# A hybrid attention and recurrence layer in fp32: which copy the weight casts stand behind, and a new written order for head pairs and gates

## The chip, the cores and the metric

The kernel runs on one core of a Trainium2 chip. A core has five engines with queues of their own, each working through its instructions in order: TensorE (PE; PEld is its weight load), VectorE (DVE), ScalarE (ACT), GpSimd (POOL) and SyncE (SP). DMA transfers are issued from some of these queues and run beside them. On-chip memory is SBUF; matmuls write to banks of PSUM. The metric is the device time of one execution in microseconds (us); the median of three runs before the change is 1459.82 us.

## The reference

One layer, on an input `x` of 1024 tokens by 1024 channels, float32 throughout. A stick-breaking attention (8 heads of 64) and a gated linear recurrence (HGRN2, 4 heads of 128, chunks of 64 tokens) work side by side on the same normalised input; each is projected back, weighted by a sigmoid gate per channel, and the two are added. A squared-ReLU MLP and a last norm follow.

```python
xn = rmsnorm(x, norm1_g[layer])
u = xn @ w_in[layer].astype(f32)        # 1024 x 5632 columns
q_sb, k_sb, v_sb, f_raw, i_hg, q_hg, g_hg, gate_sb, gate_hg = jnp.split(u, list(c), axis=-1)
o_sb = merge_heads(stick_breaking_attention(...))
f = lb + (1.0 - lb) * jax.nn.sigmoid(f_raw)
o_hg = hgrn2_chunkwise(silu(q_hg), k_hg, i_hg, log(f))      # per head
o_hg = merge_heads(rmsnorm(o_hg)) * jax.nn.silu(g_hg)
g_a = jax.nn.sigmoid(gate_sb + bg[:D_MODEL])
g_b = jax.nn.sigmoid(gate_hg + bg[D_MODEL:])
merged = g_a * (o_sb @ w_o_sb) + g_b * (o_hg @ w_o_hg)
h = x + merged @ w_out[layer]
a = jnp.square(jax.nn.relu(rmsnorm(h, norm2_g) @ w_ff1))
return rmsnorm(h + a @ w_ff2, final_g)
```

## The kernel before

**Arithmetic.** A float32 product is made of three matmuls on halves of reduced precision: each operand is split into a high half `h` and a low half `l`, and `three` (its matmuls are at L121) issues h·h, h·l and l·h. A split is a cast on ACT (`hi_copy`, L148) and behind it a subtraction on DVE (`lo_sub`, L153); `hi_lo` does both. For large products the blocks of the operands are added first and multiplied in fewer products (Strassen's way): so weights are not only split but summed (`sub`, L1093), and the sums are split. A product's parts are kept as "1", "2", "X", "Y" and so on.

**Two lanes.** Up to about 540 us PE works on two lists in turns. The main lane holds the attention items and, head by head, the levels of the recurrence (for each level, multiplications on DVE by `pp`, a sum operand `sl_x`, score matmuls `sl`, and a masked copy into `sc`). The fill lane is a `Stream` named `st`: a list of jobs, each with its weight units and a body that yields after every few matmuls. `hg_jobs(h)` adds the projections of a recurrence head (`wf`, `wq`, and for even heads `wi`), `g_job(j)` the gate of a pair of heads (`wgg0`, `wgg1`), `gate_job(cb)` one block of 128 columns of both channel gates (`wga0` to `wga7`).

**A raw block** (`raw_job`; `g_job` and `gate_job` are made with it) has a unit of two raw tiles. The first is split as it is (`whi`, `wlo`). The second becomes a sum by two subtractions (`sub(rb, ra, rb)` and one of half the size), and the half of the sum is split as `t`. There are two buffers for raw tiles, and two each for `whi` and `wlo`. The body: 12 matmuls into the bank `ps`; a copy of the bank to `p1` on ACT (L1178), which a DMA on ACT's queue takes to `pd`; then `st.prefetch()`, which splits the weights of the next unit and loads those of the one after; 12 matmuls into a second bank `p4`; the sum `p14`; then 12 matmuls more into `ps`, which therefore wait for the copy; and `c11`, which makes a sigmoid of it. In `profile` rows the banks are called `pgawga` and `pgqwga`, and `p1` is `p_wga`.

**What sets the order.** The engines' orders come from a scheduler that takes instructions in written order as their inputs allow. `after(a, b)` puts instruction `a` behind `b` in this order, without a semaphore between them. `hi_lo(..., hi_behind)` uses it for a cast; `prefetch` passes the last PE instruction of the fill lane as `hi_behind` for the `whi` cast, and nothing for the `t` cast. Loads on SP's queue keep their written order (`load`).

**The gates.** `gates()` writes the last products of the gates out by hand, for two pairs of the recurrence gate (`h0`, `h1`, whose tiles carry `h`) and the eight blocks of the channel gates (`v0`, `v1`, ...). While `turns["on"]` is set, every instruction on ACT and DVE stays in the order in which it is written. A `SumPair` has `load`, `sums` (three subtractions, L1093) and `casts` (ACT casts and DVE low halves, `whig`, `wlog`, `tgh`, `tgl`); `x6`, `x7`, `y5`, `y3` are products on PE, into banks `gX` and `gY`; `x7_sums`, `y5_sum`, `y3_sum` add what earlier stages stored (`pr`, `yr`, L1090); `put(i, j)` splits a quarter of a finished operand into its halves (`ahgh`, `ahgl`).

Of the kernel before, what the change touches and what calls it, by code (L numbers as in the profile page):

```python
# [10 lines left out]
F32R = mybir.dt.float32r  # L11
# [28 lines left out]
def kernel(  # L40
# [19 lines left out]
    nc = tc.nc  # L60
# [23 lines left out]
    def bank(name):  # L84
        return psum.tile([P, 512], F32, tag="p", name=name)
# [61 lines left out]
    def hi_copy(dst, src):  # L147
        return in_turn("act", nc.scalar.copy(dst, src))  # L148

    def lo_sub(dst, src, hi):  # L150
        return in_turn(
            "dve",
            nc.vector.tensor_tensor(out=dst, in0=src, in1=hi.bitcast(F32), op=ALU.subtract),  # L153
        )

    def hi_lo(h, l, src, hi_behind=None):
        after(hi_copy(h, src), hi_behind)
        return lo_sub(l, src, h)
# [241 lines left out]
    class Unit:  # L400
# [2 lines left out]
        late = False  # L403
        roomy = ()

        def split_t(self):
            pass

        def __init__(self, name, pieces, wide=False):
# [40 lines left out]
    class Stream:  # L450
# [17 lines left out]
        def late_next(self):  # L468
            return any(u.late for us, _ in self.jobs[self.pos + 1 : self.pos + 2] for u in us)

        def prefetch(self):
            nxt = []
            for us, _ in self.jobs[self.pos + 1 :]:
                nxt += [u for u in us if u.hl is None]
                if len(nxt) >= 2:
                    break
            if nxt:
                nxt[0].split(hi_behind=lanes["fill"].last)
                nxt[0].split_t()
            if len(nxt) > 1:  # L480
                nxt[1].load()

# [22 lines left out]
    st = Stream()  # L505
# [15 lines left out]
    def proj_jobs(group, acts):  # L521


        def body():
            for half in range(2):
                if half == 1 and st.late_next():
                    st.prefetch()
                for name, unit, ep in group:
                    ps = bank(f"{name}_{half}")
                    yield from proj_half(ps, unit.hl[0], acts.mov, KT, half)  # L530
                    ep(ps, half)

        return st.add([u for _, u, _ in group], body)
# [288 lines left out]

    j_hg = {}

    def hg_jobs(h):
        for key, c0, ep in (
            ("f", C_F, f_epilogue(h)),
            ("q", C_QH, silu_epilogue(h, "q")),
        ):
            u = cols_unit(f"w{key}{h}", [(W_IN, c0 + h * P, P)])  # L830
            j_hg[h] = proj_jobs([(f"pj{key}{h}", u, ep)], xn)
        if h % 2 == 0:
            j_hg[h] = i_job(h)

# [251 lines left out]
    def half(name, dt=F32):  # L1086
        return hpool.tile([P, 512], dt, tag="h", name=name)
# [42 lines left out]
    class RawUnit(Unit):  # L1130
# [18 lines left out]
            sub(rb[:, 512:], rb[:, 512:], rb[:, 0:512])  # L1149
            self.hl = [(h, l)]  # L1150

        def split_t(self):
            if len(self.hl) == 1:
                t = slot(f"{self.name}t", F32R)
                self.hl.append((t[:, 0:512], t[:, 512:]))
                hi_lo(*self.hl[1], self.raw[1][:, 512:])

    def raw_job(name, cols, pd, c11, begin=None, middle=None):
        u = RawUnit(name, cols)

        def steps_of(ps, wt, w0, half_, k0, start):
            wh, wl = u.hl[wt]
            for k in range(4):
                c = (w0 + k) * P
                xh, xl = xn.mov(k0 + k, half_)
                three(
                    ps, wh[:, c : c + P], wl[:, c : c + P], xh, xl, start and k == 0, k == 3, True
                )
                if k % 2 == 1:
                    yield  # L1170

        def body():
            p1, p14 = (half(f"{n}_{name}") for n in ("p1", "p14"))
            ps, p4 = bank(f"pga{name}"), bank(f"pgq{name}")
            if begin:
                begin()
            yield from steps_of(ps, 0, 0, 0, 0, True)
            nc.scalar.copy(p1, ps)  # L1178
            nc.scalar.dma_start(pd[:, 0, :], p1)
            if len(u.hl) == 1:  # L1180
                u.split_t()
            st.prefetch()
            yield from steps_of(p4, 1, 0, 1, 4, True)
            add(p14, p1, p4)
            if middle:
                middle()
            nc.gpsimd.dma_start(pd[:, 1, :], p14)
            yield from steps_of(ps, 0, 4, 0, 4, False)
            c11(ps)

        return st.add([u], body)

    def gate_job(cb):
# [116 lines left out]

    j_raw, j_g = [], []
    hg_jobs(1)
    j_fill = j_hg[1]
    j_g.append(g_job(0))
    hg_jobs(2)
    j_raw += [gate_job(0), gate_job(1)]
    hg_jobs(3)
    j_g.append(g_job(1))
# [3 lines left out]
    class SumPair:  # L1322
# [26 lines left out]
            sub(r1[:, s0], r1[:, s1], r0[:, s0])  # L1349
            sub(r0[:, s1], r1[:, s1], r0[:, s1])  # L1350

        def casts(self, behind=None):
            cb = self.cb
            r0, r1 = self.raw
            s0, s1 = slice(0, 512), slice(512, 1024)
            h, l = (self.tile(t, f"{t}g{cb}", F32R) for t in ("whi", "wlo"))
            after(hi_lo(h, l, r1), behind)
            self.w = {6: (h[:, s0], l[:, s0]), 3: (h[:, s1], l[:, s1])}
            h, l = (slot(f"tg{n}{cb}", F32R) for n in "hl")
            after(hi_lo(h, l, r0), behind)  # L1360
            self.w.update({5: (h[:, s0], l[:, s0]), 7: (h[:, s1], l[:, s1])})

        def split(self, behind=None):
            self.sums()
            self.casts(behind)

        def product(self, i, ps, start):
            open_block("fill")
# [73 lines left out]
    class GatePair(SumPair):  # L1442
# [18 lines left out]
        def casts(self, behind=None):  # L1461
            super().casts(behind)
            h, l = (half(f"wo{n}{self.cb}", F32R) for n in "hl")
            hi_lo(h, l, self.wo)
            self.hg = h, l

        def hg_product(self, i):
            open_block("fill")
# [63 lines left out]
    summed = [HgPair(0), HgPair(1)] + [gp[4 * i + j] for j in range(4) for i in range(2)]  # L1532

    def gates():
        h0, h1, v0, v1 = summed[:4]
        turns.update(on=True, act=None, dve=None)
        h1.load_sums()
        h1.roomy, v0.roomy = ("whi", "wlo"), ("raw",)
        h1.sums()
        h0.first_quarter()  # L1540
        h1.casts()
# [48 lines left out]
        v0.y3_gate()  # L1590
        v0.late_half()
        v0.early_half()
        for v, n, m in zip(summed[3:], summed[4:] + [None], summed[5:] + [None] * 2):
            if v is not v1:
                v.x6()
            v.y5()
            if n:
                n.split(v.u2_sum)
# [12 lines left out]
            v.y3_sum()  # L1611
            v.y3_gate()
            v.early_half()
# [568 lines left out]
    for i, it in enumerate(items):  # L2182
# [12 lines left out]
        def between():  # L2195
            if before:
                values(*before)

        r = turn(*it, between)
# [163 lines left out]
```

## Time and profile before

| what | value |
|---|---|
| median of 3 runs | 1459.82 us (1459.38 to 1459.86) |
| the profiled execution's own time | 1457.9 us |
| its span, first to last instruction | 1456.1 us |
| mean granted TensorE clock | 0.997 |
| instructions in the profile | 19929 |
| PE waits for `p_wga` (L1178) | 4.8 us in 2 waits, the longest 4.3 us |

The profile is of one execution. Times in its rows are microseconds from the first instruction; L12 is line 12 of the kernel. A row of the timeline has start, duration, engine, line, operation, written and read tiles with buffer numbers left out (so `wga5r` is both raw tiles of that block), and in brackets how long the engine stood before it and what ended that. Matmuls are pipelined, so their durations overlap: the distance of starts is what one costs.

### The profile page before, as it was taken

To read this page: it belongs to the slowest core of one execution; us is meant where nothing else is said; L and a number is where in the kernel's file an instruction comes from. 1 tells how busy PE (TensorE), PEld (TensorE's weight loads), DVE (VectorE), ACT (ScalarE), POOL (GpSimd) and SP (SyncE) were. 2 spreads that over 40 slices of the span, in tenths; PEclk is the share of its full clock that TensorE was granted. 3 is DMA by queue.
4 is the path that set the end of the run, shared out by engine and by line. 5 is a ranking of instruction groups with operands and counts; after the bars stand their busy time and mean duration, and the time that the engine had idled before them with its cause. 6 is when DMAs were issued, how large, how long until landed. Compare 5 with 4: busy or idle time off the path is not lost. (4 is left out here: it accounts for less than half of the span.)

```text
span 1456.1 us, 19929 instructions
## 1 busy us (share of the span) xinstructions
PE 1433.2 (98%) x7418; PEld 1215.7 (83%) x7418; DVE 1114.2 (77%) x1587; ACT 685.4 (47%) x1184; POOL 127.7 (9%) x321
## 2 busy tenths in 40 slices
PE   8999999999999899999999999999999999999997
PEld 8889988988988788888888877888888888888886
DVE  6699898698577898897777798666666757768765
ACT  7566666552323344432344764444444533523433
POOL 3021111000000030000010300000000000000041
PEclk9999999999999999999999999999999999999999
DMA  7144255003034585645579413444445975676724
GB/s 207 34 120 90 57 111 109 16 23 97 20 116 108 160 224 181 203 151 179 177 265 297 159 44 131 158 158 147 158 159 180 352 261 191 247 278 244 281 102 178
DMA packets 162216, 232.01 MB, mean 159 GB/s; under 512 B 25564, under 2 KB 96264, under 8 KB 162120
## 3 DMA queue, kind: packets, MB, share of 16 engines
q1 hardware_dynamic: 146408, 187.22, 38.3%
q0 software_dynamic: 11536, 35.92, 9.5%
q10 hardware_dynamic: 4176, 7.60, 1.4%
q8 instruction: 58, 0.95, 0.3%
q14 instruction: 38, 0.31, 0.1%
HBM read 166.48 MB, written 64.23 MB: 158 GB/s over the span
## 5 line engine op out<-in xcount | busy, mean ns | idle before, releaser
L148 ACT CAST whid<-w 128x1024 fp32r<-128x1024 f32 x31 | 32.6, 1053 | 154.5 <-PE pm L121 89.9
L698 DVE TENSOR_TENSOR_SCAN rm<-rm,bits 128x511 f32<-128x511 f32 (+7 forms) x72 | 87.1, 1218 | 14.2 <-ACT rm L676 12.6
L121 PE MATMUL pm<-wlod,sh 128*128 128x512 f32 x248 | 96.6, 389 | 0.2 <-DVE wlod L153 0.2
L121 PE MATMUL pm<-whid,sl 128*128 128x512 f32 x248 | 96.5, 389 | 0.0
L121 PE MATMUL pm<-whid,sh 128*128 128x512 f32 x248 | 96.5, 389 | 0.0
L153 DVE TENSOR_TENSOR wlod<-w,whid 128x1024 fp32r<-128x1024 f32 x31 | 37.9, 1222 | 57.0 <-ACT whid L148 56.9
L121 PE MATMUL pm<-th,sl 128*128 128x512 f32 x200 | 77.8, 389 | 0.0
L121 PE MATMUL pm<-tl,sh 128*128 128x512 f32 x200 | 77.8, 389 | 0.0
L121 PE MATMUL pm<-th,sh 128*128 128x512 f32 x200 | 77.8, 389 | 0.0
L153 DVE TENSOR_TENSOR sl<-sa,sh 128x1024 fp32r<-128x1024 f32 x56 | 68.2, 1217 | 2.2 <-ACT sh L148 2.2
L148 ACT CAST wTh<-pw 128x128 fp32r<-128x128 f32 (+3 forms) x96 | 44.4, 487 | 48.7 <-PE pw L124 43.9
L148 ACT CAST sh<-sa 128x1024 fp32r<-128x1024 f32 x56 | 57.2, 1046 | 12.1 <-DMA sa<-ad 12.1
L153 DVE TENSOR_TENSOR wTl<-pw,wTh 128x512 fp32r<-128x512 f32 (+3 forms) x96 | 50.7, 547 | 9.9 <-ACT wTh L148 5.4
L121 PEld LDWEIGHTS pm<-wlod,sh 128*128 128x128 f32 x248 | 46.6, 188 | 10.3 <-DVE wlod L153 0.6
L121 PEld LDWEIGHTS pm<-whid,sh 128*128 128x128 f32 x248 | 46.5, 187 | 9.7
L121 PEld LDWEIGHTS pm<-whid,sl 128*128 128x128 f32 x248 | 46.6, 188 | 9.5
L2006 POOL TENSOR_SCALAR fss<-fss 128x1 f32<-128x1 f32 x8 | 4.4, 551 | 566.8 <-ACT fsc L2001 566.3
L161 DVE TENSOR_TENSOR bt<-bt,rm 128x511 f32<-128x511 f32 (+7 forms) x72 | 48.9, 685 | 4.4 <-ACT bt L679 0.3
L121 PE MATMUL pX<-sqh,t1l 128*128 128x512 f32 x128 | 50.1, 391 | 1.1 <-DVE t1l L153 1.1
L121 PE MATMUL pX<-sqh,t1h 128*128 128x512 f32 x128 | 50.1, 391 | 1.0 <-DVE a L1090 0.9
L676 ACT ACTIVATE rm<-z 128x511 f32<-128x511 f32 (+6 forms) x96 | 47.6, 503 | 5.2 <-DVE bt L161 1.8
L121 PE MATMUL pX<-sql,t1h 128*128 128x512 f32 x128 | 50.0, 390 | 0.0
(971 smaller groups left out, 4587.1 us busy)
## 6 DMA issues: line engine op xcount, KB each, us to landing
w<-in_w_ff_dram SPq DMA_DIRECT2D x72, 512.0 KB, 5.0
sa<-ad SPq DMA_DIRECT2D x56, 512.0 KB, 6.5
ad<-a SPq DMA_DIRECT2D x32, 256.0 KB, 2.0
ad<-s SPq DMA_DIRECT2D x16, 512.0 KB
tw<-in_w_out_dram POOLq DMA_DIRECT2D x6, 1024.0 KB, 7.7
x<-in_x_dram SPq DMA_DIRECT2D x8, 512.0 KB, 9.4
xnl<-xnh POOLq DMA_DIRECT2D x8, 512.0 KB, 10.5
pr<-pd SPq DMA_DIRECT2D x8, 512.0 KB, 6.5
```

Source lines behind the costliest of these rows:

```text
L121: return pe(nc.tensor.matmul(*a, **k))
L148: return in_turn("act", nc.scalar.copy(dst, src))
L153: nc.vector.tensor_tensor(out=dst, in0=src, in1=hi.bitcast(F32), op=ALU.subtract),
L161: return dve(nc.vector.tensor_tensor(out=out, in0=a, in1=b, op=ALU.mult))
L676: nc.scalar.activation(rm[:, s0 + c0 - 1 : s0 + m - 1], z[:, c0:m], AF.Sigmoid, scale=-0.125)
L698: sc = nc.vector.tensor_tensor_scan(out=rr, data0=rr, data1=bits[:, 1024 - nk + a : 1024 - nk + b][:, ::-1], initial=rm[:, b : b + 1] if i ...
L2006: nc.gpsimd.tensor_scalar(out=ssq, in0=ssq, scalar1=1.0 / D, scalar2=EPS, op0=ALU.mult, op1=ALU.add)
```

## The change

It has three parts.

1. **The next block's casts.** `prefetch` and `split_t` take an instruction to stand behind. `raw_job` passes the copy to `p1`, so the next unit's `whi` cast and its `t` cast, where there is one, both come behind the running block's copy in ACT's order.
2. **Head pairs.** `hg_jobs` takes a function to call between its two projections. The first `g_job` is added there, so `wgg0` stands behind `wf2` in the fill lane and on the load queue: `wf1, wq1, wf2, wgg0, wq2, wi2` for `wf1, wq1, wgg0, wf2, wq2, wi2`.
3. **The first gate blocks.** `casts` is split into `casts_hi` (ACT) and `casts_lo(n)` (DVE), and `gates()` is written in another order: the two puts `(0, 0)` ahead of `v0.sums` and `h0.x6`, `v1`'s casts ahead of `h1.x7`, `v0.y5` and `v0.y5_sum` ahead of `h1.late_times` and `h1.y3`, the other puts of `h1` earlier, and `v2`'s load, sums and casts ahead of the loop.

```diff
-        def prefetch(self):
+        def prefetch(self, behind=None):
...
             if nxt:
-                nxt[0].split(hi_behind=lanes["fill"].last)
-                nxt[0].split_t()
+                nxt[0].split(hi_behind=behind or lanes["fill"].last)
+                nxt[0].split_t(behind)
...
-    def hg_jobs(h):
+    def hg_jobs(h, between=None):
...
             j_hg[h] = proj_jobs([(f"pj{key}{h}", u, ep)], xn)
+            if between:
+                between()
+                between = None
...
-        def split_t(self):
+        def split_t(self, hi_behind=None):
...
-                hi_lo(*self.hl[1], self.raw[1][:, 512:])
+                hi_lo(*self.hl[1], self.raw[1][:, 512:], hi_behind)
...
-            nc.scalar.copy(p1, ps)
+            copied = nc.scalar.copy(p1, ps)
...
-            st.prefetch()
+            st.prefetch(copied)
...
-    j_g.append(g_job(0))
-    hg_jobs(2)
+    hg_jobs(2, lambda: j_g.append(g_job(0)))
...
-        def casts(self, behind=None):
+        def casts_hi(self):
...
+            for _, r, h in self.lows:
+                hi_copy(h, r)
+
+        def casts_lo(self, n, behind=None):
+            for _ in range(n):
+                after(lo_sub(*self.lows.pop(0)), behind)
...
         h1.first_quarter()
+        h0.put(0, 0)
+        h1.put(0, 0)
         v0.sums()
         h0.x6()
-        h0.put(0, 0)
-        h1.put(0, 0)
-        v0.casts()
+        v0.casts_hi()
+        v0.casts_lo(3)
...
         h0.early_times()
+        v1.casts_hi()
         h1.x7()
         h1.x7_sums()
+        h0.put(1, 0)
         h1.late_sigmoids()
-        h0.put(1, 0)
+        v1.casts_lo(1)
         v0.x6()
+        v1.casts_lo(2)
+        v1.load_sums()
+        v0.y5()
+        v0.y5_sum()
         h1.late_times()
-        v1.load_sums()
-        v1.casts()
         h1.y3()
         h1.y3_sum()
-        v0.y5()
-        v0.y5_sum()
         h1.put(1, 1)
+        h1.put(0, 1)
...
         v0.x7_sums()
+        h1.put(1, 0)
         v0.x7_gates()
-        h1.put(0, 1)
-        h1.put(1, 0)
         v0.y3()
-        turns["on"] = False
-        summed[4].load()
+        v2.load()
...
         v0.late_half()
+        v2.sums()
         v0.early_half()
+        v2.casts_hi()
+        turns["on"] = False
...
+            if n is v2:
+                v2.casts_lo(3, v.u2_sum)
+            elif n:
+                n.split(v.u2_sum)
```

Lines of the changed kernel behind the first of these places stand 3 lower in the file, those of the gates 9 to 18. The first place is ACT in the fourth raw block, while `wga4` runs and `wga5` is prepared. `o1` is a finished operand of the recurrence, `asbh0` a high half of the attention's output, `sc2` a masked copy of scores, `gd3` and `pd4` are DMAs. Before:

```order
L1205 DMA gd3_114<-g1_3_5398 128x512
L148 CAST wga5t_5456<-wga5r1_5344 128x512
L1052 ACTIVATE o1_4991<-pot1_1_5411,prm_91 128x512
L148 CAST asbh0_5508<-osb0_960 128x1024
L1178 COPY p1_wga4_5401<-pgawga4_5403 128x512
L148 CAST wga5whi_5450<-wga5r0_5342 128x1024
L986 COPY sc2_4959<-sl2_5_5423 32x8x32 x2
L1179 DMA pd4_107<-p1_wga4_5401 128x512
```

And now:

```order
L1208 DMA gd3_114<-g1_3_5398 128x512
L1055 ACTIVATE o1_4991<-pot1_1_5411,prm_91 128x512
L1181 COPY p1_wga4_5401<-pgawga4_5403 128x512
L148 CAST wga5whi_5450<-wga5r0_5342 128x1024
L989 COPY sc2_4959<-sl2_5_5423 32x8x32 x2
L1182 DMA pd4_107<-p1_wga4_5401 128x512
L148 CAST wga5t_5456<-wga5r1_5344 128x512
L148 CAST asbh0_5508<-osb0_960 128x1024
```

The copy `p1_wga4` stood behind the casts `wga5t` and `asbh0`; now both stand behind it, and `wga5whi` right behind it as before. The second place is DVE at the first gate blocks, ahead of PE's product `x7` of `h0`. `guh0` is the sum after which PE may go on writing `gXh`. Before:

```order
L153 TENSOR_TENSOR tglh1_6374<-wgh1r0_6356,tghh1_6373 128x1024
L161 TENSOR_TENSOR o2_5564<-o2_5564,g11r1_6362 128x512
L1093 TENSOR_TENSOR wg0r0_6377<-wg0r0_6377 128x512
L1093 TENSOR_TENSOR wg0r1_6378<-wg0r1_6378,wg0r0_6377 128x512
L1093 TENSOR_TENSOR wg0r0_6377<-wg0r1_6378,wg0r0_6377 128x512
L1090 TENSOR_TENSOR guh0_6412<-prh0_6174,gXh0_6399 128x512
L153 TENSOR_TENSOR ahgl0_6415<-o0_4340,ahgh0_6414 128x512
L153 TENSOR_TENSOR ahgl2_6419<-o2_5564,ahgh2_6418 128x512
```

And now:

```order
L153 TENSOR_TENSOR tglh1_6372<-wgh1r0_6356,tghh1_6371 128x1024
L161 TENSOR_TENSOR o2_5564<-o2_5564,g11r1_6362 128x512
L153 TENSOR_TENSOR ahgl0_6397<-o0_4340,ahgh0_6396 128x512
L153 TENSOR_TENSOR ahgl2_6401<-o2_5564,ahgh2_6400 128x512
L1096 TENSOR_TENSOR wg0r0_6377<-wg0r0_6377 128x512
L1096 TENSOR_TENSOR wg0r1_6378<-wg0r1_6378,wg0r0_6377 128x512
L1096 TENSOR_TENSOR wg0r0_6377<-wg0r1_6378,wg0r0_6377 128x512
L1093 TENSOR_TENSOR guh0_6420<-prh0_6174,gXh0_6407 128x512
```

The two low halves `ahgl0` and `ahgl2` stood behind `guh0` and now stand ahead of the sums of `wg0`, and so ahead of `guh0`. On PE, the 12 matmuls of `gY0` moved ahead of the 12 of `gYh1`'s second half. The third place is DVE at the end of the attention's last items, where the fill lane goes from head 1 to head 2. `wTl` are low halves of attention weights that PE waits for, `sd0_l` and `sl0` belong to head 0's recurrence. Before:

```order
L153 TENSOR_TENSOR wTl7_1_0_3838<-pw7_2_0_3841,wTh7_1_0_3837 128x3x128
L153 TENSOR_TENSOR sd0_l_3943<-sd0_x_3941,sd0_h_3942 128x1024
L790 TENSOR_SCALAR k1_3779<-k1_3779,oml_93 128x512
L793 TENSOR_SCALAR pp1_3778<-pp1_3778,oml_93,lb_92 128x512
L153 TENSOR_TENSOR wTl7_2_0_3792<-pw7_4_0_3861,wTh7_2_0_3791 128x4x128
L153 TENSOR_TENSOR wTl7_2_4_3794<-pw7_4_1_3868,wTh7_2_4_3793 128x128
L161 TENSOR_TENSOR q0_3074<-q0_3074,pp0_2854 128x512
L153 TENSOR_TENSOR wTl7_1_0_3838<-pw7_3_0_3885,wTh7_1_0_3837 128x4x128
L769 TENSOR_TENSOR osb3_3314<-po7_2_3892,ot7_2_3905 64x256
```

And now:

```order
L153 TENSOR_TENSOR wTl7_1_0_3836<-pw7_2_0_3839,wTh7_1_0_3835 128x3x128
L153 TENSOR_TENSOR sd0_l_3949<-sd0_x_3947,sd0_h_3948 128x1024
L153 TENSOR_TENSOR wf2l0_3871<-wf2r0_3684,wf2h0_3870 128x1024
L790 TENSOR_SCALAR k1_3777<-k1_3777,oml_93 128x512
L793 TENSOR_SCALAR pp1_3776<-pp1_3776,oml_93,lb_92 128x512
L153 TENSOR_TENSOR wTl7_2_0_3790<-pw7_4_0_3859,wTh7_2_0_3789 128x4x128
L153 TENSOR_TENSOR wTl7_2_4_3792<-pw7_4_1_3866,wTh7_2_4_3791 128x128
L161 TENSOR_TENSOR q0_3074<-q0_3074,pp0_2854 128x512
L153 TENSOR_TENSOR wTl7_1_0_3836<-pw7_3_0_3891,wTh7_1_0_3835 128x4x128
L1096 TENSOR_TENSOR wgg0r1_3876<-wgg0r0_3874,wgg0r1_3876 128x1024
L769 TENSOR_TENSOR osb3_3314<-po7_2_3898,ot7_2_3911 64x256
```

The low half `wf2l0` came into the row ahead of two of the `wTl`, and the sum `wgg0r1`, which before stood earlier than the rows shown, now stands right behind the last `wTl`. On SP's queue the load of `wf2r0` now stands ahead of those of `wgg0`.

More of the change, by code (lines that the diff above doesn't have):

```diff
@@ L1150, in split, with split_t @@
             self.hl = [(h, l)]
-        def split_t(self):
+        def split_t(self, hi_behind=None):
             if len(self.hl) == 1:
@@ L1356, in casts @@
             h, l = (self.tile(t, f"{t}g{cb}", F32R) for t in ("whi", "wlo"))
-            after(hi_lo(h, l, r1), behind)
+            self.lows = [(l, r1, h)]
             self.w = {6: (h[:, s0], l[:, s0]), 3: (h[:, s1], l[:, s1])}
             h, l = (slot(f"tg{n}{cb}", F32R) for n in "hl")
-            after(hi_lo(h, l, r0), behind)
+            self.lows.append((l, r0, h))
             self.w.update({5: (h[:, s0], l[:, s0]), 7: (h[:, s1], l[:, s1])})
+            for _, r, h in self.lows:
[3 more added lines that the diff above has]
+                after(lo_sub(*self.lows.pop(0)), behind)
         def split(self, behind=None):
             self.sums()
-            self.casts(behind)
+            self.casts_hi()
+            self.casts_lo(len(self.lows), behind)
         def product(self, i, ps, start):
@@ L1459, in load_sums, with casts_hi @@
                 load(t.rearrange("p (k t) -> p k t", k=2), d[cb])
[L1461 to L1465, printed above, removed]
+        def casts_hi(self):
+            super().casts_hi()
+            h, l = self.hg = tuple(half(f"wo{n}{self.cb}", F32R) for n in "hl")
+            hi_copy(h, self.wo)
+            self.lows.append((l, self.wo, h))
         def hg_product(self, i):
@@ L1534, in gates @@
     def gates():
-        h0, h1, v0, v1 = summed[:4]
+        h0, h1, v0, v1, v2, v3 = summed[:6]
         turns.update(on=True, act=None, dve=None)
+        h1.roomy, v0.roomy = ("whi", "wlo"), ("raw",)
         h1.load_sums()
-        h1.roomy, v0.roomy = ("whi", "wlo"), ("raw",)
         h1.sums()
         h0.first_quarter()
-        h1.casts()
+        h1.casts_hi()
+        h1.casts_lo(2)
         v0.load()
@@ L1596, in gates @@
             v.y5()
+            if n is v2:
+                v2.casts_lo(3, v.u2_sum)
+            elif n:
+                n.split(v.u2_sum)
             if n:
-                n.split(v.u2_sum)
                 n.load_sums()
```

## The prediction

> **What bounds the kernel now.** I read the page first: the span and the engines' busy shares.
>
> ```profile
> span 1456.1 us, 19929 instructions
> PE 1433.2 (98%) x7418; PEld 1215.7 (83%) x7418; DVE 1114.2 (77%) x1587; ACT 685.4 (47%) x1184; POOL 127.7 (9%) x321
> ```
>
> TensorE (PE) is the bound: 1456.1 − 1433.2 = 23 us in all are not PE work. The change leaves every matmul in, so it can win only idle time of PE and time at a lower clock. Next the view of waits, for PE alone (what it waited for: total us, times, longest).
>
> ```profile
> PE pgawga L121 <- ACT p_wga L1178: 4.8, 2, 4.3
> ...
> PE gY L121 <- DVE pr L1090: 0.5, 1, 0.5
> ```
>
> The first row is the wait that the change is about: a gate block's first PSUM bank waits until ScalarE (ACT) has copied it out to `p_wga`. It occurs twice, once 4.3 us long. Third, the timeline around that one, block 4 (start, duration, engine, line, operation).
>
> ```profile
> 495.37 0.62 ACT L148 CAST wga5t<-wga5r 128x512 fp32r<-128x512 f32 x1 [8.16 <-DVE wga5r L1093]
> 495.90 0.68 ACT L1052 ACTIVATE o<-pot,prm 128x512 f32<-128x512 f32 x1
> 496.48 1.03 ACT L148 CAST asbh<-osb 128x1024 fp32r<-128x1024 f32 x1
> 497.41 0.59 ACT L1178 COPY p_wga<-pgawga 128x512 f32<-128x512 f32 x1
> ```
> ```profile
> 493.39 1.22 DVE L1093 TENSOR_TENSOR wga5r<-wga5r,wga5r 128x1024 f32<-128x1024 f32 x1 [2.95 <-DMA wga5r<-in_w_in_dram]
> 494.65 0.69 DVE L1093 TENSOR_TENSOR wga5r<-wga5r 128x512 f32<-128x512 f32 x1
> 499.78 0.41 DVE L161 TENSOR_TENSOR q<-q,pp 128x256 f32<-128x256 f32 x1
> ```
> ```profile
> 493.15 0.39 PE L121 MATMUL pgqwga<-xnl,wga4t 128*128 128x512 f32 x1
> 493.38 0.39 PE L121 MATMUL pgqwga<-xnh,wga4t 128*128 128x512 f32 x1
> 498.05 0.79 PE L121 MATMUL pgawga<-xnh,wga4whi 128*128 128x512 f32 x1 [4.29 <-ACT p_wga L1178]
> ...
> 500.91 0.80 PE L121 MATMUL sl<-q,k 128*64 128x64 f32 x10
> ```
>
> ACT stood for 8.16 us at a cast of the *next* block (`wga5t`), since its input, a sum on VectorE (DVE), waited for a DMA until 493.39. Three operations and 2.6 us later came the copy that PE needed. Matmuls of this form start 493.38 − 493.15 = 0.23 us apart; the six from 498.05 to 500.91 took 2.86 us instead of 1.38. The view of windows tells why (stretch, length, busy us and instructions of PE, PEld, DVE, ACT, POOL; then granted clock, mean DMA engines' share, GB/s).
>
> ```profile
> 6.00:9.40 3.40, 1.28 (x10) 0.88 (x9) 1.63 (x3) 2.19 (x3) 1.50 (x3) 1.00 1.18 295
> 9.40:12.80 3.40, 3.40 (x19) 3.40 (x18) 3.38 (x7) 3.32 (x9) 0.00 (x0) 0.50 1.05 386
> ...
> 494.10:497.50 3.40, 0.00 (x0) 0.00 (x0) 1.90 (x3) 2.13 (x4) 0.00 (x0) 1.00 0.00 0
> 497.50:500.90 3.40, 2.85 (x6) 1.82 (x6) 3.35 (x8) 2.05 (x5) 0.00 (x0) 0.50 0.74 231
> ```
>
> A stretch without PE work is followed by one at half clock. So the stall cost 4.29 + (2.86 − 1.38) = 5.8 us.
>
> **The change, part by part.** *Block 4.* No operation is removed; ACT's `p1` copy now comes ahead of the next block's casts, `wga5t` and `asbh0` behind it. Of what stood ahead, only the 0.68 us `o` activation remains, whose operand PE wrote long before ACT ran it. The bank is full before the 12 matmuls of the second bank, 12 × 0.23 = 2.8 us that end at 493.6, so by 490.8; ACT, free then, has copied it (0.59) at about 492, and the whole 5.8 us goes. What is late next: `wga5whi`, cast from the first raw tile without the sum, waits for the same DMA behind the copy, but block 5 begins only six matmuls and a score group later. Queued behind that cast on ACT are two copies of tail scores and the block's DMA of `p1`; no PE instruction soon waits for them. Bounds: −5.8 to −4.0 (1.8 of new wait, the second rival). I take **−5.8**.
>
> *The other gate blocks* get the same order. Only one of them had a visible wait, block 2:
>
> ```profile
> 469.58 1.05 ACT L148 CAST wga3whi<-wga3r 128x1024 fp32r<-128x1024 f32 x1 [7.20 <-DVE k L161]
> 470.54 0.58 ACT L1178 COPY p_wga<-pgawga 128x512 f32<-128x512 f32 x1
> 471.17 0.50 PE L121 MATMUL pgawga<-xnh,wga2whi 128*128 128x512 f32 x1 [0.47 <-ACT p_wga L1178]
> ```
>
> The cast ahead of the copy took 1.05 us and PE waited 0.47, so the swap removes all of it: **−0.5** (to 0, if the copy too is held by what held the cast). In blocks 5 to 7 the casts come later in ACT's order, so their low halves come later on DVE:
>
> ```profile
> 508.11 1.21 DVE L153 TENSOR_TENSOR wga6wlo<-wga6r,wga6whi 128x1024 fp32r<-128x1024 f32 x1
> ```
> ```profile
> L121 PE MATMUL pgawga<-xnh,wga6wlo x8: 389/389/396, 513.8 to 522.9; 128*128 128x512 f32 x8
> ```
>
> `wga6wlo` is done at 509.3 and first used at 513.8: 4.5 us of cover. PE now arrives 5.8 us sooner. If the raw tile's load, issued when the block before frees a buffer, moves along with PE, the cover stays; if nothing moves, 5.8 − 4.5 = 1.3 us are missing, and block 7's chain is the same. Since DVE no longer holds other work behind `wga3r`'s and `wga5r`'s waits, I expect most of it to move. Bounds 0 to +1.5; nothing here can gain, as neither block waited. I take **+0.3**.
>
> *Gates.* The puts `h0.put(0,0)` and `h1.put(0,0)` (the `ahgl` subtractions) now stand ahead of `v0.sums` (the `wg0r` subtractions) in the written order, all ahead of `guh0`:
>
> ```profile
> 598.25 0.69 DVE L161 TENSOR_TENSOR o<-o,g11r 128x512 f32<-128x512 f32 x1
> 598.85 0.68 DVE L1093 TENSOR_TENSOR wg0r<-wg0r 128x512 f32<-128x512 f32 x1
> 599.57 1.29 DVE L1093 TENSOR_TENSOR wg0r<-wg0r,wg0r 128x512 f32<-128x512 f32 x2
> 600.78 0.68 DVE L1090 TENSOR_TENSOR guh<-prh,gXh 128x512 f32<-128x512 f32 x1
> 601.38 1.29 DVE L153 TENSOR_TENSOR ahgl<-o,ahgh 128x512 fp32r<-128x512 f32 x2
> ```
> ```profile
> 600.86 0.39 PE L121 MATMUL gYh<-gsh,tglh 128*128 128x512 f32 x1
> 601.52 0.50 PE L121 MATMUL gXh<-gsh,tghh 128*128 128x512 f32 x1 [0.27 <-DVE guh L1090]
> ```
>
> DVE runs here without a gap, so the two `ahgl` (1.29 us) push `guh0` from 600.78 to about 602.05, its end to 602.7. PE, which could go on at 601.09 and went on at 601.52 (0.43 late), goes on at about 602.8: +1.3 us. Against that, `v0.y5_sum` moves ahead of `h1.y3` and 12 matmuls of `gY0` with it, so the later wait for `pr` (0.5 in the waits above) has 12 matmuls, 2.8 us, more cover and goes: −0.5. Sum **+0.8**; bounds −0.9 (both waits go, if the sums' input lets DVE run ahead) to +1.3 (the later wait stays).
>
> *Head pairs.* The first gate-pair block `wgg0` goes behind `wf2`, in the PE order and on SP's load queue.
>
> ```profile
> 298.28 0.37 SPq L129 DMA_DIRECT2D wgg0r<-in_w_in_dram  x1
> ```
> ```profile
> 318.16 0.68 DVE L153 TENSOR_TENSOR wTl<-pw,wTh 128x512 fp32r<-128x512 f32 x1
> 336.48 1.21 DVE L153 TENSOR_TENSOR wf2l<-wf2r,wf2h 128x1024 fp32r<-128x1024 f32 x1
> 341.86 0.42 DVE L161 TENSOR_TENSOR q<-q,pp 128x256 f32<-128x256 f32 x1
> ```
> ```profile
> 317.51 0.39 PE L121 MATMUL po<-wTl,V 128*128 128x256 f32 x1 [1.34 <-DVE wTl L153]
> ...
> 343.20 1.95 PE L121 MATMUL sl<-q,k 128*128 128x128 f32 x16
> ```
> ```profile
> DMA to landing us min/median/max: 3.9/3.9/3.9
> ```
> ```profile
> DMA to landing us min/median/max: 5.3/5.3/5.3
> ```
>
> DVE loses the `wgg0r` sums (1.22 + 0.69, durations of `wga5r`'s) that ran near 303 and gains `wf2l` (1.21) ahead of the `wTl` that PE waits for at 317.51: that stall stays as it is within 0.3 us. The second `wgg0` raw tile was loaded at 298.28; it now gets its buffer only behind `wf2l`, about 316. By the last two rows (landing of the raw tiles `wi2r` and `wq2r`) it is there at 319.9 to 321.3. Its sum stands on DVE right behind the last `wTl`, which ends at 318.8, so all of DVE's queue waits 1.1 to 2.5 us. That and the sums (1.9) less `wf2l` (1.2) make the multiplies of head 0's levels 1.8 us late at the lower end. The scores at 343.20 start 0.9 behind the end of their multiply (342.28): 1.8 − 0.9 = 0.9 if nothing of it is made up; about twenty short operations of masks stand between on DVE, that the scheduler now puts elsewhere in part, so I take half, **+0.5**; bounds −0.3 (the level of 317.51) to +2.3 (0.9 + 1.4 for a landing of 5.3).
>
> *Sum:* −5.8 − 0.5 + 0.3 + 0.8 + 0.5 = −4.7 us. The profiled execution took 1457.9 us (span 1456.1 and 1.8 around it), 1.9 under the median of 1459.82; 1457.9 − 4.7 = 1453.2, by the median **1455.1**.
>
> **The clock rule.** In the rows above the 6.00 window had 1.28 us of PE work, and the next ran at 0.50: a window need not be empty. The Trainium skill, "TensorE: Matmul & The Clock Gate", section "What's actually happening", says that the clock falls to half after at least one *idle* window of about 3.4 us; the windows from 494.10 agree, the one from 6.00 had work and does not. By the page the gates' new 1.7 us wait costs no clock and the sum stands; by the row at 6.00, with 2.1 us idle, it may, which is the first rival.
>
> **Rivals.** *1, the gate wait halves the clock.* 602.8 − 601.1 = 1.7 us without work may fall into one window (half of the positions of a 1.7 us gap in 3.4 us). One window at half speed costs 3.4/2 = 1.7 us: 1455.1 + 1.7 = 1456.8. Against it: 1.7 idle is less than the 2.1 of the only row. Chance 0.10.
>
> *2, the wait is replaced.* `wga5r` lands at 493.39 whatever ACT does, if its buffer comes free no sooner. DVE then ends the two sums at 495.3, and the level-5 multiplies (four of them 0.41 us long, as at 499.78) at about 496.9; PE reaches the score matmuls that stood at 500.91 at 495.1 and waits 1.8. With 1 us more in blocks 6 and 7: 1455.1 + 2.8 = 1457.9. This is also how the change could fail to do what it says. For it: the DMA wait of 2.95. Against it: those multiplies now stand ahead of the `t` subtraction, and the sums' tile should be loaded sooner. Chance 0.16.
>
> *3, slower.* The `wgg0` tile lands late and DVE, in order, blocks. Another 512 KB transfer of this kernel, by the page's DMA issues, takes long:
>
> ```profile
> xnl<-xnh POOLq DMA_DIRECT2D x8, 512.0 KB, 10.5
> ```
>
> At 10.5 the tile lands at 326.5 and DVE stands 7.7 us instead of 1.1. The heads' term becomes 1.8 − 1.1 + 7.7 − 0.9 = 7.5, and 1.7 for the clock: −4.7 − 0.5 + 9.2 = +4.0, 1463.8. It decides from a landing of 6.5 us (slower at all), measurably from 9.4. Against it: the two rows of that neighbourhood are 3.9 and 5.3. Chance 0.16, all other ways to lose with it.
>
> **How the numbers follow.** The forecast case has 0.58; its own range, by its terms' bounds, is 1452 to 1457. 0.2% of 1459.82 is 2.9 us, about what a measurement of this kernel can tell from no change: faster ends at 1456.9, slower begins at 1462.7. Faster: 0.58 + half of rival 1 (0.05) + the third of rival 2 in which its wait is shorter (0.05) = 0.68. Same: 0.05 + 0.11 + the milder end of rival 3 (0.03) = 0.19. Slower: 0.13. Range: low 1451.8 (the gates at −0.9 instead of +0.8, heads and blocks at 0, and 0.8 less), high 1460.0, which takes in rivals 1 and 2 and leaves out rival 3.
>
> **What would show it.** The wait of `pgawga` for `p_wga` is gone, and the clock stays 1.00 from 480 to 500; if not, the first step is wrong. A wait of `gXh` for `guh` of about 1.7 us and none of `gY` for `pr`: the gates. A DMA wait on DVE at `wgg0r` near 319, and a small wait of `sl` for `q`: the heads. Waits of `pgawga` for `wga6wlo` or `wga7wlo`, or of `sl` near 495, would be rival 2. The forecast fails if PE's idle time does not fall by about 3 us.

## The result and the profile after

The changed kernel takes 1451.39 us (median of 4 runs, 1451.17 to 1452.69) against 1459.6 us (4 runs, 1458.33 to 1459.86): a ratio of 0.9947, 95% interval 0.993 to 0.9965. It is faster, and by more than the 1455.1 forecast: the median lies 0.4 us under the low end of the range. The profiled execution took 1451.17 us, its span is 1449.3 us, 6.8 us shorter than before.

The page of the changed kernel, its busy shares:

```profile
span 1449.3 us, 19944 instructions
PE 1431.0 (99%) x7418; PEld 1215.2 (84%) x7418; DVE 1114.2 (77%) x1587; ACT 686.2 (47%) x1184; POOL 131.8 (9%) x321
```

PE has the same 7418 matmuls. Its waits (what it waited for: total us, times, longest):

```profile
PE warm L121 <- POOL ident masks.py:199: 2.2, 1, 2.2
PE xnt L124 <- DVE x L576: 1.8, 2, 1.0
PE po L121 <- DVE wTl L153: 1.8, 3, 1.2
PE pX L121 <- DVE t1l L153: 1.2, 2, 0.6
PE gXh L121 <- DVE guh L1093: 0.9, 1, 0.9
...
```

The wait of `pgawga` for `p_wga` and that of `gY` for `pr` are gone; the wait of `gXh` for `guh` went from 0.3 to 0.9. Block 4 on ACT and DVE, where before the copy stood behind `wga5t` until 497.41:

```profile
487.05 0.69 ACT L1055 ACTIVATE o<-pot,prm 128x512 f32<-128x512 f32 x1 [1.11 <-PE pot L124]
488.44 0.59 ACT L1181 COPY p_wga<-pgawga 128x512 f32<-128x512 f32 x1 [0.70 <-PE pgawga L121]
488.92 1.05 ACT L148 CAST wga5whi<-wga5r 128x1024 fp32r<-128x1024 f32 x1
...
491.26 0.62 ACT L148 CAST wga5t<-wga5r 128x512 fp32r<-128x512 f32 x1 [0.66 <-DVE wga5r L1096]
```
```profile
489.28 1.23 DVE L1096 TENSOR_TENSOR wga5r<-wga5r,wga5r 128x1024 f32<-128x1024 f32 x1 [1.72 <-DMA wga5r<-in_w_in_dram]
490.54 0.69 DVE L1096 TENSOR_TENSOR wga5r<-wga5r 128x512 f32<-128x512 f32 x1
```

The copy now runs as soon as PE has filled the bank. And the sum of `wga5r` still waits for its DMA, 1.72 us, but starts at 489.28, 4.1 us earlier than before, when PE at this place is only 1.3 us earlier. The window view of those 20 us shows no idle time and the full clock (busy us of PE, PEld, DVE, ACT, POOL, then clock):

```profile
480.00:500.00 20.00, 20.00 (x136) 16.56 (x136) 16.59 (x32) 8.71 (x14) 1.15 (x2) 1.00 0.55 168
```

The clearest reading comes from the same matmul in two traces. PE does the same work in all kernels of this study, so the difference of its start times, taken stretch by stretch, says where time was won. The columns: the two reorders of the heads near 317; block 2 near 470; block 4 near 495; the gates at `gXh` near 601 and at `gY` near 626; and the sum of these. (What stands ahead of the heads and behind the gates is left out: between these traces the first differs by up to 1.8 us, the second by up to 2.0.) The row of the forecast has the prediction's terms.

| trace, against the first trace of before | heads | block 2 | block 4 | `gXh` | `gY` | sum |
|---|---|---|---|---|---|---|
| forecast (and +0.3 in blocks 6 and 7) | +0.5 | −0.5 | −5.8 | +1.3 | −0.5 | −4.7 |
| changed kernel | −0.13 | −1.16 | −5.88 | +0.59 | −0.81 | −7.40 |
| changed kernel, second trace | −0.13 | −1.16 | −5.88 | +0.16 | −0.81 | −7.83 |
| kernel before, second trace | 0.01 | +0.26 | −0.21 | −0.41 | −0.04 | −0.39 |
| casts alone (first part) | 0.02 | −1.16 | −5.88 | +0.34 | −0.04 | −6.72 |
| heads alone (second part) | −0.13 | −0.49 | −0.10 | +0.07 | −0.03 | −0.69 |
| gates alone (third part) | 0.02 | −0.10 | −0.29 | +0.97 | −0.81 | −0.22 |
| first cast alone | 0.02 | −1.16 | −2.12 | −0.23 | −0.04 | −3.52 |
| second cast alone | 0.01 | −0.79 | −4.77 | −0.09 | −0.05 | −5.69 |
| puts back | −0.15 | −1.16 | −5.88 | −0.55 | −0.81 | −8.56 |
| puts back, `wf2` later | −1.29 | −1.16 | −5.88 | +0.43 | −0.81 | −8.71 |
| puts back, `wf2` later, second trace | −1.29 | −1.16 | −5.90 | −0.56 | −0.81 | −9.72 |
| longer wait at the gates | −0.15 | −1.16 | −5.90 | +5.87 | −0.81 | −2.15 |

The second trace of before says how far a column can be trusted: a few tenths.

### The profile page after: what moved, and what is told of

It is laid out like the page before. It is cut to its first block, busy times and chain, and to the rows that moved or that the text cites. A ratio compares the mean times of both kernels' runs of the same rounds, so it can differ in the third digit from the quotient of the medians.

```text
span 1449.3 us, 19944 instructions
## 1 busy us (share of the span) xinstructions
PE 1431.0 (99%) x7418; PEld 1215.2 (84%) x7418; DVE 1114.2 (77%) x1587; ACT 686.2 (47%) x1184; POOL 131.8 (9%) x321
```

## The experiments

My theory was that the whole gain is the copy's place in ACT's order. The rival was that the new orders of heads and gates, which move DVE's work, have a share in it.

**The three parts, one at a time.** Each is the hunks of that part alone on the kernel before.

Casts alone:

```diff
-                nxt[0].split(hi_behind=lanes["fill"].last)
-                nxt[0].split_t()
+                nxt[0].split(hi_behind=behind or lanes["fill"].last)
+                nxt[0].split_t(behind)
...
-            st.prefetch()
+            st.prefetch(copied)
```

> Only the casts behind the copy of the running block's first bank; head pairs and gates as before. Theory A (the change's gain is this part alone): PE ends block 2 about 1.1 us and block 4 about 5.9 us sooner, both waits of pgawga for p_wga gone, nothing else moves before the gates: about -7.0 us by the trace. Theory B (the new order of head pairs or gates has a share in the two places, since it moves DVE's work): less than 6 us. At the first gate block DVE should run ahead of PE by the 0.8 us that it did after the whole change, so the wait of gXh for guh (0.27 before) should be gone or nearly: A adds up to -0.4 there.

Measured 1451.74 us against 1457.82 us (ratio 0.9955, 0.9941 to 0.997). Blocks 2 and 4 gain the same 1.16 and 5.88 us as in the whole change, so the first part explains them alone. The second half of the expectation was wrong. The gates' wait did not go; it grew, and `gY`'s stayed:

```profile
PE gXh L121 <- DVE guh L1090: 0.6, 1, 0.6
PE gY L121 <- DVE pr L1090: 0.5, 1, 0.5
```

PE came to the gates 7 us sooner, DVE did not by as much: `guh` began 5.6 us sooner (595.22 against 600.78), and ahead of it DVE stood 1.87 us until the raw tile `wgh1r` landed and 1.0 us until `wg0r` did.

Heads alone:

```diff
-    j_g.append(g_job(0))
-    hg_jobs(2)
+    hg_jobs(2, lambda: j_g.append(g_job(0)))
...
```

> Only the first gate-pair block behind wf2. Theory A: within 0.3 us of before; PE's stall at wTl near 317 0.1 shorter as after the whole change, DVE waits about 1.1 us for wgg0r near 319, no new wait of PE, both waits for p_wga as before. Theory B: a part of the 1.1 us at block 2 is seen here. The prediction's own step said +0.5 (up to +2.3) with a wait of PE at sl for q.

Measured 1456.53 us against 1457.82 us (0.9986, 0.9977 to 0.9996): a small gain. Near 317 PE gains the 0.13 us; no wait for the scores `sl` appears. Half a microsecond comes at block 2: the wait of `pho` for `hon` there (0.1 us idle in the trace before) is gone, and `p_wga`'s is shorter. The rival expected a part here, but that the new order of the heads is its cause is not shown. Block 2 follows the moment at which DVE can begin the sum of `wga3r`, that is when this tile lands. Taken against PE's own shift just ahead of the block, the sum begins 0.50 us sooner here and block 2 gains 0.49; but in the second trace of before it begins 0.25 later and block 2 loses 0.26, and with the second cast alone (below) it begins 0.77 sooner and block 2 gains 0.79, the heads unchanged in both. In the whole change this half is no extra, since the casts alone win all of block 2.

Gates alone:

```diff
         h1.first_quarter()
+        h0.put(0, 0)
+        h1.put(0, 0)
         v0.sums()
         h0.x6()
-        h0.put(0, 0)
-        h1.put(0, 0)
...
```

> Only the redone order of the gates. The prediction's step: gXh waits for guh 1.3 us longer than the 0.43 before (start to start), gY's wait of 0.64 to 0.8 goes: +0.5 to +0.8 in all. If DVE reaches the gates sooner only because block 4's stall is gone, that is what comes here; if the new order itself lets DVE run ahead, the wait grows by 0.6 as after the whole change, and the sum is -0.2.

Measured 1457.69 us against 1457.82 us (1.0, 0.9991 to 1.001): no change. This is the case the prediction's gates term described, and the term is nearly right: `gXh` +0.97 (forecast +1.3), `gY` −0.81 (forecast −0.5).

```profile
PE gXh L121 <- DVE guh L1090: 1.3, 1, 1.3
```

**The two casts of the first part.** The `t` cast free as before, only `whi` behind the copy:

```diff
-                nxt[0].split(hi_behind=lanes["fill"].last)
+                nxt[0].split(hi_behind=behind or lanes["fill"].last)
                 nxt[0].split_t()
...
```

> Of the first part, only the whi cast stands behind the copy; the t cast is free as before. Theory A (two casts, two places: whi cost block 2, t and asbh cost block 4): block 2's 1.1 us go, block 4's stall of 4.3 with its half-clock 1.5 stays, about -1.1 us in all. Rival: the whi cast is what holds the copy in block 4 too (it waits for the same tile's DMA); then more than 3 us are gained here.

Measured 1452.89 us against 1457.82 us (0.9962, 0.9947 to 0.9977). Block 2 went as expected. Block 4 did not: it gained 2.1 us although `wga5t` and `asbh` still stood ahead of the copy on ACT:

```profile
491.99 0.62 ACT L148 CAST wga5t<-wga5r 128x512 fp32r<-128x512 f32 x1 [4.63 <-DVE wga5r L1093]
492.51 1.04 ACT L148 CAST asbh<-osb 128x1024 fp32r<-128x1024 f32 x1
493.46 0.58 ACT L1178 COPY p_wga<-pgawga 128x512 f32<-128x512 f32 x1
```
```profile
494.08 0.50 PE L121 MATMUL pgawga<-xnh,wga4whi 128*128 128x512 f32 x1 [1.98 <-ACT p_wga L1178]
```

So a second cause was at work. SP's queue of this run and of before show it, in that order:

```profile
472.14 2.35 SPq L129 DMA_DIRECT2D wga4r<-in_w_in_dram  x2
484.12 0.99 SPq L129 DMA_DIRECT2D wga5r<-in_w_in_dram  x2
```
```profile
474.93 2.18 SPq L129 DMA_DIRECT2D wga4r<-in_w_in_dram  x2
486.47 1.00 SPq L129 DMA_DIRECT2D wga5r<-in_w_in_dram  x2
```

The loads of `wga4r` and `wga5r` were issued 2.8 and 2.35 us sooner. Of this, 0.5 us is an earlier start of this execution and 1.16 is what PE had won at block 2, so that the loads ran ahead of PE by 1.1 and 0.7 us. And the sum of `wga5r` began at 490.00 instead of 493.39, so from issue to sum it took about 1 us less. It took 5.67 to 5.96 us in all eight traces with the `whi` cast behind the copy and 6.75 to 6.92 in the five without. In those five the DMA `pd` of the copied bank goes out 1.1 us ahead of this load, in the eight at least 4 us ahead; that this is the reason is not shown. The last 0.6 us of the 2.3 by which the wait is shorter are ACT's own: `o`, which before stood between `wga5t` and `asbh`, had run at 486.66. A raw tile is loaded when the block before has given its buffer free, that is after its low halves are subtracted on DVE (`wga3wlo` ends at 472.11 here and at 474.90 before, just ahead of the loads of `wga4r`). In block 2 the swap of a cast and a copy on ACT changed DVE's order too, and the chain of buffers then ran ahead through blocks 3 and 4.

The other way round, the `t` cast behind the copy and `whi` where it was:

```diff
                 nxt[0].split(hi_behind=lanes["fill"].last)
-                nxt[0].split_t()
+                nxt[0].split_t(behind)
...
```

> Of the first part, only the t cast stands behind the copy; the whi cast is placed as before, in blocks 2 and 4 ahead of the copy. Theory C (after the run with the first cast alone, which cut block 4's wait from 4.3 to 2.0 us: two causes there, ACT's order and a chain of loads that started 2.3 us sooner): block 2 stays as before (1.1 us lost); the chain of loads stays late, wga5r issued near 486.5; at block 4 the copy stands only behind wga5whi, which waits for the first raw tile (landing some 6 us after its issue, near 492.5), so PE waits 0.5 to 1.5 us and loses no clock: about -4.5 us at block 4. If the t cast alone were the cause, all of 5.9 goes; if the load chain were, 2.3 or less.

Measured 1452.65 us against 1456.6 us (0.9978, 0.9964 to 0.9991). Block 2 did not stay as before: it gained 0.79 us with `whi` still ahead of its copy, as the sum of `wga3r` began 0.77 us sooner. At block 4 the load moved only along with PE (`wga5r` at 486.59 against 486.47, in an execution that started 1.15 us later and had won 0.79 by then), yet the copy is in time: it stands behind `wga5whi` alone, which needs only the first raw tile, and that landed by 491.

```profile
491.08 1.05 ACT L148 CAST wga5whi<-wga5r 128x1024 fp32r<-128x1024 f32 x1 [1.70 <-DMA wga5r<-in_w_in_dram]
492.03 0.58 ACT L1178 COPY p_wga<-pgawga 128x512 f32<-128x512 f32 x1
```
```profile
496.12 1.08 PE L121 MATMUL sl<-q,k 128*64 128x64 f32 x10 [0.64 <-DVE q L161]
```

Block 4 gains 4.77 of 5.88. What is missing is a new wait, of the scores for multiplies that stand on DVE behind the late sum: the prediction's second rival, at 0.64 us of idle time (1.0 by the starts) instead of 1.8. In the whole change it is absent, and there `wga5r` is loaded 2.9 us sooner than before (483.57 against 486.47), 1.3 of which PE is sooner too. So ACT's order alone removes 4.77 us of the stall, the first cast with its sooner load 2.12, and together they remove all of it.

**The gates.** The two puts behind `v0.sums` and `h0.x6` again, all else as changed:

```diff
-        h0.put(0, 0)
-        h1.put(0, 0)
         v0.sums()
         h0.x6()
+        h0.put(0, 0)
+        h1.put(0, 0)
```

> The changed kernel with the two puts (0,0) behind v0.sums and h0.x6 again. The prediction's step for the gates (each ahgl subtraction costs guh0 0.6 us, 1.3 with the wait for its cast): the wait of gXh for guh, 0.85 us idle, 1.0 by distance of starts, goes wholly, and nothing else moves: -1.0 us against the changed kernel by the trace. If the wait has another cause (the sums wg0r late by their load), it stays.

Measured 1450.33 us against 1456.6 us (0.9964, 0.9948 to 0.998). PE does not wait at `gXh` any more; by PE's starts that is 1.14 us against the changed kernel (+0.59 to −0.55). DVE of this run and of the changed kernel, in that order:

```profile
585.30 1.29 DVE L1096 TENSOR_TENSOR wgh1r<-wgh1r,wgh1r 128x512 f32<-128x512 f32 x2 [1.58 <-DMA wgh1r<-in_w_in_dram]
...
592.52 0.68 DVE L1093 TENSOR_TENSOR guh<-prh,gXh 128x512 f32<-128x512 f32 x1
```
```profile
585.64 1.29 DVE L1096 TENSOR_TENSOR wgh1r<-wgh1r,wgh1r 128x512 f32<-128x512 f32 x2 [1.88 <-DMA wgh1r<-in_w_in_dram]
...
594.24 0.68 DVE L1093 TENSOR_TENSOR guh<-prh,gXh 128x512 f32<-128x512 f32 x1
```

From the sum of `wgh1r` to `guh` DVE takes 7.22 us here and 8.60 us in the changed kernel: the puts cost 1.38 us of DVE's queue, as the prediction had it (1.3). The rest is when that row starts. It starts when the raw tile `wgh1r` lands.

The same, and `wf2`'s split deferred until 24 matmuls of `wq1` are written (a step is 6 matmuls, and the split comes with the fourth; the expectation says 12):

```diff
+                if units[0].name == "wq1":
+                    self.gen = self.behind_steps(body(), 3)
+                    return
                 self.prefetch()
             self.gen = body()
+
+        def behind_steps(self, steps, n):
+            for i, s in enumerate(steps):
+                if i == n:
+                    self.prefetch()
+                yield s
...
```

> The run before, and wf2's split deferred until 12 matmuls of wq1 are written, so that wf2l stands on DVE behind the wTl that PE waits for at 317. If DVE's queue length is what PE waits for there, the wait of 1.2 us falls by the 1.1 us that wf2l takes; if it is the chain of transposes, casts and low halves itself, it stays. Costs: the wgg0 tile is loaded some 6 us later (DVE waits in order near 325), with at most 1 us of wait at the scores of head 0. Sum -1.0 from the puts and -1.1 to 0 here against the changed kernel.

Measured 1448.84 us against 1456.6 us (0.9952, 0.9935 to 0.9968). `wf2l` was what PE waited for at 317, through DVE's order: the heads gain 1.29 us instead of 0.13. But 0.98 of it is lost again at the gates:

```profile
PE gXh L121 <- DVE guh L1102: 0.7, 1, 0.7
PE po L121 <- DVE wTl L153: 0.3, 1, 0.3
```
```profile
585.55 1.29 DVE L1105 TENSOR_TENSOR wgh1r<-wgh1r,wgh1r 128x512 f32<-128x512 f32 x2 [3.07 <-DMA wgh1r<-in_w_in_dram]
...
592.77 0.68 DVE L1102 TENSOR_TENSOR guh<-prh,gXh 128x512 f32<-128x512 f32 x1
```

In this execution the tile kept DVE waiting for 3.07 us, where it was 1.58 in the run before: PE came 1.15 us sooner and the tile's loads were issued 1.2 us sooner, but the sum began 0.25 us later; why the landing took longer is not shown. The wait on DVE for `wgg0r` that was expected near 325 did not come (its sum runs at 334.49 without one).

**A longer wait at the gates.** For the first rival, two repeated operations (the maximum of a tile with itself, which changes nothing) stand on DVE ahead of `v0.sums` in the changed kernel:

```diff
+        t = h0.p[:, 512:1024]
+        for c in (t, t[:, 0:256]):
+            dve(nc.vector.tensor_tensor(out=c, in0=c, in1=c, op=ALU.max))
         v0.sums()
```

> The changed kernel with two repeated operations on DVE (maximum of a tile with itself, 512 and 256 columns, 0.6 and 0.35 us) ahead of v0.sums: the wait of gXh for guh grows from 0.85 to about 1.8 us, the size that the prediction gave it. Rival 1: if that stretch without work lies in one 3.4 us window, the next window runs at 0.50 and 1.5 us more are lost (2.4 in all against the changed kernel). Otherwise +0.95 us, clock 1.00. By the pauses seen so far (2.1 of 3.4 idle halved the clock, 1.3 did not) 1.8 lies between.

One run of 1455.97 us. The wait became 3.3 us, not 1.8: DVE lost 1.06 us to the two operations, and 1.45 more because the sum of `wgh1r`, for which DVE waited again, began at 587.09 instead of 585.64. The windows around the wait:

```profile
593.20:596.60 3.40, 0.93 (x5) 0.43 (x3) 3.33 (x6) 0.34 (x1) 0.00 (x0) 1.00 0.73 252
596.60:600.00 3.40, 2.52 (x6) 2.04 (x7) 3.40 (x5) 2.17 (x3) 0.00 (x0) 0.51 0.78 249
600.00:603.40 3.40, 3.40 (x9) 2.63 (x9) 3.19 (x6) 0.00 (x0) 0.00 (x0) 0.50 0.34 139
603.40:606.80 3.40, 3.40 (x16) 2.79 (x16) 1.64 (x4) 1.23 (x2) 0.00 (x0) 0.99 0.86 304
```

The clock was halved for two windows. PE lost 5.3 us there against the changed kernel, 2.5 by the longer wait and 2.8 by the clock. So a wait of this kind can cost the clock, as the first rival had it; a wait of 1.8 us at this place was not tested.

**Both kernels again, and the best version beside them.** On one chip the kernel before (one trace more), the changed kernel, and the version with the puts back and `wf2` later.

> The kernel before once more, for a second trace of it. Executions of it spread over 8 us on the last chip, those of the kernels with the casts behind the copy over 1.4 to 2. If block 4's wait is what varies (it hangs on the landing of wga5r), this trace shows another length of it than 4.3 us, and the same PE times everywhere else within 1 us; if not, the spread is elsewhere (the start, the MLP).

> The changed kernel beside the version with the puts back and wf2 later, on one chip: 6.5 to 8 us under the kernel before, and 1.3 us over that version, as the traces of both say. Its PE times stand within 0.5 us of its first trace everywhere, since no wait of it hangs on the landing of wga5r.

> 1.0 to 1.5 us under the changed kernel. The gates' wait for guh follows the landing of the raw tiles wgh1r, for which DVE waited 4.0 us in its first trace, so it may be anything from 0 to 0.9.

Before: 1459.16 us in this run, 1458.02 in the median of its 13 runs beside the others, which spread from 1452.77 to 1459.11. Its block 4 stall is 3.88 us here instead of 4.29, with the half clock again, and the rest agrees within half a microsecond; so this trace shows no cause for the spread of 6 us, which stays open. Changed: 1451.32 (ratio 0.9959, 0.9949 to 0.997), 6.7 us under the kernel before, as expected, with the same gains at block 2 and block 4 to the hundredth. Its gates' wait is 0.4 us instead of 0.9, as `wgh1r`'s sum begins sooner (584.92), and one wait of 0.55 in the MLP near 1130 (0.85 by the starts) is new: the expectation "within 0.5 us everywhere" failed there. Puts back and `wf2` later: 1449.38 (0.995, 0.9933 to 0.9968), 1.9 us under the changed kernel beside it, where 1.0 to 1.5 was expected. It waits neither at 317 (0.05 us idle) nor at `gXh`. Its median is the lowest of the three.

## Why the prediction was right, and where it was not

The mechanism was right for the two terms that gain at the copy, and the sum was too small by 2.7 us in the traces (−7.4 between the start and the MLP, forecast −4.7): the net losses that it put at the gates, the heads and blocks 6 and 7 did not come.

- *Block 4, −5.8 forecast, −5.88 measured.* The stall and its half clock both went. The size agrees because the whole stall went, and for that two causes were needed. The step gave one, the copy's place on ACT; the runs with one cast each show a second, loads that ran ahead and landed sooner (first cast alone: 2.1 us of gain with the old order of `t`). The second rival, a replaced wait at the scores, was real, 0.64 us with the second cast alone, and was kept away by that sooner load. The prediction's argument against it ("the sums' tile should be loaded sooner") was the right one, though it gave no reason there.
- *Block 2, −0.5 forecast, −1.16 measured.* Mis-sized. I counted 0.47 us of idle time in a row. By the starts of the matmuls on both sides PE lost 0.69 there, and a second wait just ahead, of `pho` for `hon`, went too, because the casts' new place let DVE do `hon` ahead of the sum of `wga3r`, for which DVE had stood 5.18 us. The quoted row of ACT named its releaser as DVE; I didn't ask what DVE had been waiting for. Nor was it the cast alone that kept the copy: on ACT's queue the DMA `hgd` stood ahead of both, and went out at 469.22, when its input `sg`, behind `hon` on DVE, was done at 469.18 (the case for which the prediction's bound went to 0).

```profile
469.22 0.33 ACTq L1220 DMA_DIRECT2D hgd<-sg  x1
```

  In the changed kernel it went out at 464.21, and the copy ran at 465.76, as soon as PE had filled the bank.
- *Blocks 6 and 7, +0.3 forecast, 0 measured.* No wait of `pgawga` is left; the loads moved along with PE.
- *Gates, +0.8 forecast, −0.22 measured.* The step's size of 1.38 us for the puts was right, and `gY` gave 0.8 instead of 0.5 (again, idle time instead of the distance of starts). What failed is "DVE runs here without a gap" as the ground on which `guh0` was timed. DVE had no gap at that place, but 4.7 us ahead of the first row quoted there it had waited 2.58 us for `wgh1r` to land; its timing hangs on that tile, and PE's does not. In the five traces of the changed kernel and of the versions with the puts back, the sum of `wgh1r` starts at 583.87 to 585.64, and the wait for `guh` is 0 to 0.9. The tile `wg0r` can do the same: DVE stood 0.7 us for it in the second trace of before and 1.0 with the casts alone.
- *Heads, +0.5 forecast, −0.13 measured.* The wait on DVE for `wgg0r` came as forecast, 1.13 us at 319.89:

```profile
319.89 1.23 DVE L1096 TENSOR_TENSOR wgg0r<-wgg0r,wgg0r 128x1024 f32<-128x1024 f32 x1 [1.13 <-DMA wgg0r<-in_w_in_dram]
...
336.09 0.68 DVE L1096 TENSOR_TENSOR wgg0r<-wgg0r 128x512 f32<-128x512 f32 x1
```

  But the second sum was put off to 336.09 and the masks' operations were spread out, so the multiplies of the next level kept their cover: a delay on DVE's queue was taken for a delay of PE. The third rival did not occur: the tile landed at 319.9, the lower of the two landings that the prediction used.
- *The first rival.* In the changed kernel the wait was 0.9 us and cost no clock:

```profile
593.90:597.30 3.40, 2.55 (x11) 1.95 (x11) 3.40 (x5) 2.37 (x3) 0.00 (x0) 1.00 0.89 269
597.30:600.70 3.40, 3.40 (x17) 2.81 (x16) 3.37 (x6) 0.00 (x0) 0.00 (x0) 1.00 1.00 366
```

The medians differ by 8.2 us, the two profiled executions by 6.7, the medians of the later runs of both kernels by 6.7. The prediction was summed against one profiled execution that was 1.9 us under the median, and that much of the distance to 1451.39 lies there.

## What to carry to other kernels

When a wait is removed by changing an in-order queue, follow the buffers as well: the operation that now runs earlier frees its input earlier, and the loads behind it can move ahead too, here those of the next two blocks. Take the price of a wait from the distance of starts, and look one step behind the releaser that a row names. Before timing a busy engine from its place in the order, find the last DMA for which it waited: here that landing, and not DVE's rate alone, set when `guh` was done.

## What the runs showed of the hardware

A window of 3.4 us need not be empty of PE work for the clock to fall. (The windows here are laid so that the granted clock changes at their edges.) Windows with 0.93 us of work (above), 1.28 us (in the trace before, at 6.00), 1.42 us (first cast alone) and 1.57 us (changed kernel, near its start) were followed by half clock; windows with 1.65 us (heads alone), 2.13 us (gates alone) and 2.55 us (changed kernel, above) were not. In this order, first cast alone, changed kernel, heads alone and gates alone:

```profile
491.90:495.30 3.40, 1.42 (x6) 1.04 (x6) 2.72 (x9) 3.28 (x6) 0.00 (x0) 1.00 0.19 46
495.30:498.70 3.40, 3.40 (x20) 2.57 (x20) 3.40 (x4) 1.96 (x3) 0.00 (x0) 0.50 0.61 185
```
```profile
6.84:10.25 3.41, 1.57 (x13) 1.29 (x13) 2.52 (x4) 1.85 (x5) 1.23 (x2) 1.00 1.09 323
10.25:13.66 3.41, 3.41 (x19) 3.41 (x18) 3.41 (x10) 3.41 (x9) 0.00 (x0) 0.50 1.06 391
```
```profile
492.76:496.17 3.41, 1.65 (x8) 1.03 (x6) 1.92 (x2) 0.45 (x1) 0.00 (x0) 1.00 0.18 69
496.17:499.58 3.41, 1.19 (x5) 1.01 (x6) 2.38 (x4) 3.40 (x7) 0.00 (x0) 1.00 0.34 100
499.58:502.99 3.41, 3.41 (x21) 2.55 (x20) 3.41 (x8) 0.33 (x1) 0.34 (x1) 0.50 0.41 139
```
```profile
599.40:602.80 3.40, 2.13 (x10) 1.46 (x9) 3.37 (x5) 2.16 (x3) 0.00 (x0) 1.00 0.85 268
602.80:606.20 3.40, 3.40 (x17) 2.80 (x16) 3.37 (x6) 0.36 (x1) 0.00 (x0) 1.00 0.98 335
```

The Trainium skill, "TensorE: Matmul & The Clock Gate", section "What's actually happening", has the fall after at least one idle window of about 3.4 us. The rows differ: in these traces the limit lies between 1.57 and 1.65 us of PE work in a window, a little under half of it, as far as the modelled busy time tells. So it matters where a wait falls. A wait of 2.0 us in one window was enough to pay for it, 1.26 us was not; and of the wait of 3.98 us with the heads alone, which spanned two windows, only the second cost the clock. Once halved, a window with 2.52 us of work did not bring the clock back (the 596.60 row), one with 2.85 us did (before, at 497.50).
